# Moving two input loads and two dozen DRAM-to-DRAM copies in a decoder block: the embedding input ahead of the second merge gate, precomputed weight sums into the attention stages and late MLP1

## The chip, the cores and the metric

The kernel runs on one core of one Trainium2 chip. The metric is device time in microseconds (us) of one execution; lower is better.

## The reference, cut to what matters

One layer of a decoder trunk, batch 1, 512 tokens, width 1024, everything in float32:

```python
h = rmsnorm(x, ln1)
hq, hk, hv, hr, ha, hatt, hgate = split(h @ w_in)
# A: gated linear attention (4 heads, chunks of 64); B: dilated attention, 3 groups of 4 heads
o      = gla(...) * gla_gn * silu(hr);      y_gla = o @ w_o_gla
o_att  = softmax-weighted sum of 3 groups;  y_att = o_att @ w_o_attn
mix = (sigmoid(gA) * y_gla + sigmoid(gB) * y_att) @ w_out
x = x + mix
x = x + square(relu(rmsnorm(x, ln2) @ w_mlp1)) @ w_mlp2
x = x + sigmoid(rmsnorm(x, ln3) @ w_pg) * (p @ w_pp)
return rmsnorm(x, ln_f)
```

The last term but one, `p @ w_pp`, is the embedding product: `p` (512 x 256) does not depend on anything else, and its transpose is the input `pT`.

## The kernel before, in words

**Products.** Every weight is cut into operands of 128 x 1024 floats (512 KB). A product in full precision is made of three float32r matmuls: each operand and each activation is split into a high part (`hi`, rounded by ScalarE) and a low part (`lo` = value - hi, on VectorE), and hi*hi, hi*lo and lo*hi are added up in PSUM. Nearly all products are done by a seven-product scheme (Strassen-Winograd): `strassen` for the narrow ones and `wide` for the wide ones, where each of the seven stages has a sum of weight blocks (A11, S1, S2, A12, S3, S4, A22) and a sum of activation blocks (B11, T1, T2, B21, T3, B22, T4) as its operands. In `wide` each weight sum comes in two operands (`.0`, `.1`) of twelve matmuls each.

**Stages.** TensorE works through this order: q0, k0, q1, k1, q2, k2 (attention scores), v12, v0 (attention values), gq, gk, gv (linear attention), oa (attention output), r (the silu gate), gb and ga (the first and the second merge gate), og (`w_o_gla`, the linear-attention output projection), pp0 (first half of `p @ w_pp`), wo (`w_out`), pp1, m1q0 to m1q7 (MLP1), m2 (MLP2), pg. Attention, linear attention and other small work is woven in between matmuls.

**Order of the work.** The order in which instructions are issued is written out by hand: `tc.manual_schedule()` keeps each engine's instructions in program order. `run` emits matmuls in pieces, and after each piece `step` takes one closure from the list `later` (work on ScalarE and VectorE, first in, first out; `rest` is an empty one) and, at a pace, one turn of a generator from `side`. So an entry in `later` decides where a piece of work stands in the queues of ScalarE and VectorE.

**Weights.** `fetch` keeps two operands ahead of TensorE: for operand i it makes `lo`, for i+1 `hi`, and for i+3 it calls `prepare`, which issues the load on SyncE's queue (line 263). A weight sum that isn't a plain block is made by the transfers: a load, and then an accumulating transfer on GpSimd's queue that adds a second block (line 273, and in the product chains line 358). The accumulating transfer waits for the load and holds up what stands behind it in GpSimd's queue. In og the chain is S1, then S2 (S1 plus A11), then S4 (S2 plus A12), each by an accumulating transfer on the buffer whose low part has been made.

**Stored sums.** Twelve of MLP2's weight sums (S1 of four chunks, S3 of two, two operands each) are made ahead of time in DRAM: `store` copies a block from DRAM to DRAM on SyncE's queue (line 284) and `accumulate` adds the second block on GpSimd's queue (line 287). The generator `stores()` spreads them over 23 turns: two copies, then a copy and an accumulation in turn (each accumulation two sums behind its copy), then two accumulations. `prepare` takes a turn at every third operand of v12 and from gk on, which ends within gb.

**Embedding inputs.** After ga and ahead of og, two 128 x 512 tiles of `pT` are loaded on GpSimd's queue (line 1487), and two entries that split them are put into `later` (line 1489). pp0 reads the split tiles after og.

**Tiles.** All 128 x 512 work tiles come from one pool of 68 buffers (`NU`); `u32()` takes one.

Of the kernel before, what the change touches and what calls it, by code (L numbers as in the profile page):

```python
# [19 lines left out]
P = 128  # L20
# [112 lines left out]
def wide_order(name):  # L133
    return TIGHT if name in TIGHTS else WIDE


def operand_order():

    names = []
    for name, kind, *_ in UNITS:  # L140
        if name == f"m2c{SEVEN[0]}.A11.0":
            names += [f"m2c{c}.{a}.{i}" for a, c in MLP2 for i in range(2)]
        elif name.startswith("m2c"):
            continue
        elif kind not in QUADS:
            names.append(name)
        elif name.endswith("A11"):
            names += [f"{name[:-3]}{a}" for a, _, _ in STAGES]
        elif name.endswith("A11.0"):
            names += [f"{name[:-5]}{a}.{i}" for a, _, _ in wide_order(name[:-6]) for i in range(2)]  # L150
    return names
# [10 lines left out]
OPERANDS = operand_order()  # L162
OPERAND = {n: i for i, n in enumerate(OPERANDS)}
# [30 lines left out]

GOPS, LAG = 4, 3

PAD, SHIFT = 128, 32

NRAW = 8
# [9 lines left out]
def block_kernel(ctx, tc, xT, x, ws, pT, wts, wha, wa2, vec, lnf, rel, onehot, ident_d, mask_d, out):  # L209
    nc = tc.nc  # L210
    V, S, TE, SY, GP = nc.vector, nc.scalar, nc.tensor, nc.sync, nc.gpsimd
# [12 lines left out]
    def u32(name="u"):  # L224
        return ar.tile([P, T], F32, tag="u", name=name)
# [11 lines left out]
    side, later = [], []  # L237
# [28 lines left out]
    def prepare(i):  # L266

        name = OPERANDS[i]
        if i % 3 == 0 and (OPERAND["v12.A11.0"] <= i < OPERAND["v0.A11"] or i >= OPERAND["gk.A11"]):
            next(spare[0], None)  # L270
        for n, a, b in EARLY.get(i, ()):
            w = raw[n] = load(a)
            GP.dma_start(w, wts[UNIT[b]], accum_op=OP.add)  # L273
        if name in UNIT or name in stored:
            raw[name] = load(name)
# [28 lines left out]
    spare = [stores()]  # L304
# [82 lines left out]
    def cols(t, c):  # L387
        return t[0][:, c], t[1][:, c]
# [8 lines left out]
    def tmaj(name, n, lhs, evac, tts=range(4), piece=PIECE, last=None, make=mmt, at=None):  # L397

        last = tts[-1] if last is None else last

        for i in range(n):
            weight(f"{name}.{i}", 0)
        for tt in tts:
            ps = make()
            mms = three(ps, [(lhs(k, tt), cols(ready[f"{name}.{k // 2}"], slice((k % 2) * 512, (k % 2 + 1) * 512)))
                             for k in range(2 * n)])
            if at:
                run(mms, piece)
                fetch(OPERAND[f"{name}.{n - 1}"] + at[tt])
            elif tt != last:  # L410
                run(mms, piece)
            else:
                for i in range(n):
                    run(mms[6 * i:6 * i + 6], piece)
                    fetch(OPERAND[f"{name}.{n - 1}"] + i + 1 + (NW - 2 - n if n < 4 else 0))
            evac(tt, ps)
# [48 lines left out]
    def wide(name, xo, finish, base=None, piece=3, extra=None, first=False):  # L465


        bank, sums = {}, {}

        def begin(m, t, n, b):  # L470
            def go():
                if base:
                    return base(m, t, n, bank[b][n], sums)
                sums[m, t, n] = u32()
                S.activation(sums[m, t, n], bank[b][n], AF.Copy, scale=-1.0 if m else 1.0)
            return go

        def end(m, t, n, b):
            return lambda: finish(m, t, n, sums.get((m, t, n)), bank[b][n])

        for i, (op, xname, b) in enumerate(wide_order(name)):
            fresh = b not in bank
            if fresh:
                bank[b] = [smt() if b == "b" else mmt() for _ in range(2)]

            def products(n, pr):
                wh, wl = weight(f"{name}.{op}.{pr // 2}")
                xh, xl = xo(xname, pr)
                c, r = slice(n * P, (n + 1) * P), slice((pr % 2) * 512, (pr % 2 + 1) * 512)
                return [(bank[b][n], l[:, c], w[:, r], fresh and not pr and not k, pr == 3 and k == 2)  # L490
                        for k, (l, w) in enumerate(((xh, wh), (xl, wh), (xh, wl)))]

            begins = [begin(*BEGINS[op][0], n, BEGINS[op][1]) for n in range(2)] if op in BEGINS else []
            if name in TIGHTS and op in ("S2", "S3"):
                for n in range(2):
                    for pr in range(4):
                        run(products(n, pr), piece, shared=True)
                    later[0:0] = begins[n:n + 1]
            else:
                for pr in range(4):  # L500
                    run(products(0, pr) + products(1, pr), piece, shared=True)
                later[0:0] = begins
            if op in ENDS:
                (m, t), d = ENDS[op]
                ends = [end(m, t, n, d) for n in range(2)]
                if first:
                    later[0:0] = ends
                else:
                    later.extend(ends)
            if extra:  # L510
                extra(i)
# [21 lines left out]
    def split(x, col=None):  # L533

        return split_lo(x, split_hi(x, col), col)
# [62 lines left out]
    for k in range(KC):  # L598
        t = u32()
        SY.dma_start(t, xT[k * P:(k + 1) * P, :])  # L600
        xr.append(t)
        t = u32()
# [231 lines left out]
    def whole(m, s, ps):  # L834

        if s is None:
            s = u32()
            S.activation(s, ps, AF.Copy, scale=-1.0 if m else 1.0)
        else:
            add(m, s, s, ps)  # L840
        return s
# [495 lines left out]
    q2 = heads("q2", HD_SCALE, True)  # L1337
# [7 lines left out]
    v0 = values("v0")  # L1345
# [3 lines left out]
    gk = heads("gk", 1.0)  # L1349
    gv = {}  # L1350
# [11 lines left out]
    def evac_oa(j):  # L1362
        def put(tt, ps):
            y = u32()
            S.activation(y, ps, AF.Copy)
            S.dma_start(y_dram[4 * j + tt], y)
        return lambda tt, ps: later.append(lambda: put(tt, ps))

    for j in range(2):
        tmaj(f"oa{j}", 2, lambda k, tt: cols(oa[k], slice(tt * P, (tt + 1) * P)), evac_oa(j), at=((1, 1, 2, 2), (1, 2, 2, 3))[j])  # L1370
    rg, tb, ga = {}, {}, {}

    def silu(m, t, n, s, ps):
        s, g = whole(m, s, ps), u32()

        def act():
            S.activation(g, s, AF.Sigmoid)

            def mult():
                V.tensor_tensor(s, s, g, op=OP.mult)  # L1380
                rg[m, 2 * t + n] = s
            later.append(mult)
        later.append(act)

    def sigmoid(res):

        def finish(m, t, n, s, ps):
            if s is None:
                o = u32()
                S.activation(o, ps, AF.Sigmoid, scale=-1.0)  # L1390
                res[m, t, n] = o
            else:
                add(m, s, s, ps)

                def act():
                    S.activation(s, s, AF.Sigmoid)
                    res[m, t, n] = s
                later.append(act)

        return finish  # L1400
# [39 lines left out]
    def room(i):  # L1440
        if i >= 4:
            limit[0] += 1

    wide("ga", xs_op, sigmoid(ga), extra=room)
    limit[0] = 99
    pace[0], ways[0] = 2048, WAYS

    def rest():
        pass

    def og_op(name, pr):
        while (name, 1) not in gparts.op:
# [3 lines left out]
    def arrange(m, t, src, blk, parts, names, rests, col=None):  # L1456

        if (m, t) == (1, 1):
            return
        later.extend([rest] * rests[m, t] + turned(src, blk, m, t, col))  # L1460
        if t:
            later.extend(turned(src, blk, 1, 1, col))
        later.extend(parts.splits([(name, g) for name in names[m, t] for g in range(2)], LAG))
# [3 lines left out]
    mixed = {}  # L1467
# [13 lines left out]
            arrange(m, t, mixed, mblk, mparts, {(0, 0): ["B11"], (0, 1): ["T1", "T2"], (1, 0): ["B21", "T3", "B22", "T4"]},  # L1481
                    {(0, 0): 12, (0, 1): 7, (1, 0): 9})

    pt = []
    for k in range(2):
        t = u32()
        GP.dma_start(t, pT[k * P:(k + 1) * P, :])
        pt.append(t)
    later.extend(lambda k=k: pt.__setitem__(k, split(pt[k])) for k in range(2))
    wide("og", og_op, onto_mix, piece=2, first=True)  # L1490

    pp_dram = dr.tile([2 * 4, P, T], F32, name="pp_dram")
# [70 lines left out]
    def quad(q):  # L1563


        def finish(m, t, s, ps):
            add(m, s, s, ps)

            def positive():
                V.tensor_scalar(s, s, 0.0, None, op0=OP.max)  # L1570

            def act():
                S.activation(s, s, AF.Square)  # L1573
                hb[q, m, t] = s

            later.extend([positive, act])

        strassen(f"m1q{q}", x1_op, finish, extra=between(q))
# [42 lines left out]

    for q in range(8):
        quad(q)
    lnb, rt3 = [], []
    x3, ss3 = {}, const.tile([P, 8], F32, name="ss3")

# [168 lines left out]
    for c in parts:  # L1795
        ps, n = mmt(), c.stop - c.start
# [99 lines left out]
```

## Time and profile before

| | |
|---|---|
| median of three runs | 943.84 us (943.05 to 944.71) |
| the profiled execution | 944.67 us, its span from first to last instruction 942.9 us |
| TensorE's mean granted clock | 0.994 |
| matmul (PE) busy | 928.4 us, 98% of the span |
| VectorE busy | 745.9 us, 79% |
| ScalarE busy | 581.3 us, 62% |
| GpSimd busy | 142.3 us, 15% |
| data moved by DMA | 183.87 MB, mean 195 GB/s |

Engines are PE (TensorE's matmuls), PEld (its weight loads), DVE (VectorE), ACT (ScalarE), POOL (GpSimd) and SP (SyncE, which issues DMAs). A row of the timeline gives start, length, engine, line, operation, tiles written and read, shape and count; in brackets stands the idle time of the engine before it, and what ended that. A row of the windows gives, for one stretch, the busy time of PE, PEld, DVE, ACT and POOL with the instruction counts, then the granted clock, the share of the 16 DMA engines that was busy, and GB/s.

### The profile page before, as it was taken

To read this page: it belongs to the slowest core of one execution; us is meant where nothing else is said; L and a number is where in the kernel's file an instruction comes from. 1 tells how busy PE (TensorE), PEld (TensorE's weight loads), DVE (VectorE), ACT (ScalarE), POOL (GpSimd) and SP (SyncE) were. 2 spreads that over 40 slices of the span, in tenths; PEclk is the share of its full clock that TensorE was granted. 3 is DMA by queue.
4 is the path that set the end of the run, shared out by engine and by line. 5 is a ranking of instruction groups with operands and counts; after the bars stand their busy time and mean duration, and the time that the engine had idled before them with its cause. 6 is when DMAs were issued, how large, how long until landed. Compare 5 with 4: busy or idle time off the path is not lost.

```text
span 942.9 us, 14591 instructions
## 1 busy us (share of the span) xinstructions
PE 928.4 (98%) x5506; PEld 822.4 (87%) x5506; DVE 745.9 (79%) x1049; ACT 581.3 (62%) x939; POOL 142.3 (15%) x187
## 2 busy tenths in 40 slices
PE   9999999999999999999979999999999999999996
PEld 8789998899998888888868889999999888888886
DVE  7698879866789388977958989877768978899764
ACT  7357546545675578887655759755556665656543
POOL 0150020030201022133112120010000112120000
PEclk9999999999999999999989999999999999999999
DMA  9574685876867959599979696656654888897302
GB/s 346 151 235 113 195 223 119 276 251 190 181 154 224 278 132 302 114 226 260 256 201 236 195 257 192 188 143 165 174 150 121 198 191 197 189 287 286 112 0 90
DMA packets 59526, 183.87 MB, mean 195 GB/s; under 512 B 7875, under 2 KB 14607, under 8 KB 59264
## 3 DMA queue, kind: packets, MB, share of 16 engines
q0 software_dynamic: 23424, 65.24, 36.2%
q1 hardware_dynamic: 32352, 113.20, 33.6%
q10 hardware_dynamic: 3680, 4.51, 1.3%
q8 instruction: 43, 0.70, 0.3%
q14 instruction: 27, 0.22, 0.1%
HBM read 174.49 MB, written 22.85 MB: 209 GB/s over the span
## 4 chain that ended last, share of the span: by engine, by line
PE 90%; DMA 4%; ACT 2%; DVE 2%; issue 1%; POOL 0%; POOLq 0%; DVEq 0%; SPq 0%; ACTq 0%
PE mmt L377 68%; PE smt L377 13%; PE mmt L646 2%; DMA y_dram<-u 2%; PE smt L1080 1%; DMA u<-in_pT_dram 1%; DMA w<-in_wts_dram 1%; PE smt L1305 1%; PE smt L1020 1%; PE smt L943 1%; PE smt L913 0%; PE smt L1037 0%; PE smt L1036 0%; PE smt L912 0%; PE smt L1026 0%
## 5 line engine op out<-in xcount | busy, mean ns | idle before, releaser
L377 PE MATMUL mmt<-hi,ur 128*128 128x512 f32 (+1 forms) x1264 | 376.8, 381 | 0.0
L340 DVE TENSOR_TENSOR lo<-w,hi 128x1024 fp32r<-128x1024 f32 x266 | 322.5, 1219 | 57.6 <-PE mmt L377 31.9
L363 ACT ACTIVATE hi<-w 128x1024 fp32r<-128x1024 f32 x266 | 277.6, 1054 | 90.2 <-PE mmt L377 23.2
L377 PE MATMUL mmt<-ur,hi 128*128 128x256 f32 (+1 forms) x1552 | 294.7, 290 | 0.0
L377 PEld LDWEIGHTS mmt<-hi,ur 128*128 128x128 f32 x1264 | 230.5, 189 | 41.3
L377 PEld LDWEIGHTS mmt<-ur,hi 128*128 128x128 f32 x1552 | 244.3, 189 | 4.2
L377 PE MATMUL mmt<-lo,ur 128*128 128x512 f32 (+1 forms) x632 | 240.3, 380 | 4.9 <-DVE lo L340 4.9
L377 PE MATMUL mmt<-ur,lo 128*128 128x256 f32 (+1 forms) x776 | 225.8, 291 | 0.0
L377 PEld LDWEIGHTS mmt<-ur,lo 128*128 128x128 f32 x776 | 146.5, 189 | 1.9
L377 PEld LDWEIGHTS mmt<-lo,ur 128*128 128x128 f32 x632 | 119.3, 189 | 27.8 <-DVE lo L340 5.6
L523 ACT ACTIVATE ur<-u 128x512 fp32r<-128x512 f32 x137 | 80.9, 626 | 61.9 <-DVE u L665 12.5
L340 DVE TENSOR_TENSOR ur<-u,ur 128x512 fp32r<-128x512 f32 x136 | 89.0, 685 | 21.8 <-ACT ur L523 21.4
L377 PE MATMUL smt<-hi,ur 128*128 128x512 f32 x320 | 99.5, 392 | 0.0
L273 POOL DMA_DIRECT2D w<-in_wts_dram x46 | 46.0, 1073 | 220.8 <-DMA w<-in_wts_dram 92.7
L516 DVE TENSOR_TENSOR u<-u,mmt 128x512 f32<-128x512 f32 (+1 forms) x90 | 55.6, 646 | 23.6 <-PE mmt L377 23.4
L377 PEld LDWEIGHTS smt<-hi,ur 128*128 128x128 f32 x320 | 60.1, 189 | 12.2
L377 PE MATMUL smt<-lo,ur 128*128 128x512 f32 x160 | 62.6, 391 | 0.0
L450 ACT ACTIVATE u<-mmt 128x512 f32<-128x512 f32 x56 | 33.2, 594 | 47.1 <-PE mmt L377 46.9
L358 POOL DMA_DIRECT2D w<-in_wts_dram x28 | 25.0, 893 | 179.0 <-DVE lo L340 89.7
L319 POOL DMA_DIRECT2D w<-in_wts_dram x14 | 12.5, 894 | 212.3 <-DVE w L316 113.4
L1573 ACT ACTIVATE u<-u 128x512 f32<-128x512 f32 x32 | 20.1, 628 | 32.3 <-DVE u L1570 32.3
L377 PEld LDWEIGHTS smt<-lo,ur 128*128 128x128 f32 x160 | 30.2, 189 | 6.6 <-DVE lo L340 0.3
(239 smaller groups left out, 871.3 us busy)
## 6 DMA issues: line engine op xcount, KB each, us to landing
w<-in_wts_dram SPq DMA_DIRECT2D x176, 512.0 KB, 5.8
w<-in_wts_dram POOLq DMA_DIRECT2D x88, 512.0 KB, 7.6
m2c_S<-in_wts_dram SPq DMA_DIRECT2D x12, 512.0 KB, 8.4
m2c_S<-in_wts_dram POOLq DMA_DIRECT2D x12, 512.0 KB, 10.8
w<-m2c_S SPq DMA_DIRECT2D x12, 512.0 KB, 4.4
u<-in_xT_dram SPq DMA_DIRECT2D x8, 256.0 KB, 5.4
u<-in_ws_dram SPq DMA_DIRECT2D x8, 256.0 KB, 5.5
v_dram<-u ACTq DMA_DIRECT2D x8, 256.0 KB, 7.0
```

What stands on the lines that cost most here:

```text
L273: GP.dma_start(w, wts[UNIT[b]], accum_op=OP.add)
L319: GP.dma_start(w, wts[UNIT[f"{q}.A21"]], accum_op=OP.add)
L340: V.tensor_tensor(lo, x, hi.bitcast(F32), op=OP.subtract)
L358: GP.dma_start(w, wts[UNIT[f"{q}.{c}{what[2:]}"]], accum_op=OP.add)
L363: S.activation(hi[:, s], w[:, s], AF.Copy, scale=1.0 if c is None else c)
L377: TE.matmul(o, lhsT=l, rhs=r, start=a, stop=b, skip_group_check=shared)
L450: S.activation(sums[c], bank[b], AF.Copy, scale=-scale if c[0] else scale)
L516: V.tensor_tensor(out, s, ps, op=OP.subtract if m else OP.add)
L523: S.activation(hi, x, AF.Copy)
L646: TE.matmul(q0ps[i], lhsT=(hi, hi, lo)[j][:, c], rhs=(xh, xl, xh)[j], start=not k and not j, stop=k == KC - 1 and j == 2)
L943: TE.matmul(pss[b // 2][:, a * 256 + lo:a * 256 + 256], lhsT=q0[h][:, b * P:(b + 1) * P], rhs=k0[h][:, (b - 1) * P + lo:(b + 1) * P], star ...
L1573: S.activation(s, s, AF.Square)
```

## The change

- The two loads of `pT` are issued as ga, the second gate, begins, in place of og's beginning. Their splits are put into `later` when og's block (1, 1) has been finished, that is behind og's fifth stage, S3; they were ahead of og.
- The turns of `stores()` are taken at other operands. A table gives a modulus for some stages, and an operand takes a turn where its number leaves a remainder of 1. Stages that are not in the table have the modulus 275, one more than the number of operands, so that one more operand takes a turn: number 1 (`k0.1`). What is left when MLP1 has been issued is issued then.
- In the silu gate `r`, the tile for the sigmoid is taken when the sigmoid is issued, and not when the block is finished. `rest` is defined earlier, which moves no instruction.

```diff
+SPARE = {"q2": 2, "v12": 3, "gk": 2, "gv": 2, "m1q4": 3, "m1q5": 2, "m1q6": 2}
...
     def prepare(i):
 
         name = OPERANDS[i]
-        if i % 3 == 0 and (OPERAND["v12.A11.0"] <= i < OPERAND["v0.A11"] or i >= OPERAND["gk.A11"]):
+        if i % SPARE.get(name.partition(".")[0], len(OPERANDS) + 1) == 1:
             next(spare[0], None)
...
     def silu(m, t, n, s, ps):
-        s, g = whole(m, s, ps), u32()
+        s = whole(m, s, ps)
 
         def act():
+            g = u32()
             S.activation(g, s, AF.Sigmoid)
...
+    pt = []
+    for k in range(2):
+        t = u32()
+        GP.dma_start(t, pT[k * P:(k + 1) * P, :])
+        pt.append(t)
     wide("ga", xs_op, sigmoid(ga), extra=room)
...
     def arrange(m, t, src, blk, parts, names, rests, col=None):
 
         if (m, t) == (1, 1):
+            if src is mixed:
+                later.extend(lambda k=k: pt.__setitem__(k, split(pt[k])) for k in range(2))
             return
...
-    pt = []
-    for k in range(2):
-        t = u32()
-        GP.dma_start(t, pT[k * P:(k + 1) * P, :])
-        pt.append(t)
-    later.extend(lambda k=k: pt.__setitem__(k, split(pt[k])) for k in range(2))
     wide("og", og_op, onto_mix, piece=2, first=True)
...
     for q in range(8):
         quad(q)
+    for _ in spare[0]:
+        pass
```

More of the change, by code (lines that the diff above doesn't have):

```diff
@@ L1370, in block_kernel, with rest @@
         tmaj(f"oa{j}", 2, lambda k, tt: cols(oa[k], slice(tt * P, (tt + 1) * P)), evac_oa(j), at=((1, 1, 2, 2), (1, 2, 2, 3))[j])
+    def rest():
+        pass
     rg, tb, ga = {}, {}, {}
     def silu(m, t, n, s, ps):
-        s, g = whole(m, s, ps), u32()
+        s = whole(m, s, ps)
         def act():
+            g = u32()
             S.activation(g, s, AF.Sigmoid)
@@ L1446, in block_kernel @@
     pace[0], ways[0] = 2048, WAYS
-    def rest():
-        pass
     def og_op(name, pr):
@@ L1623, in block_kernel @@
         quad(q)
+    for _ in spare[0]:
+        pass
     lnb, rt3 = [], []
```

## The prediction

> **What bounds the kernel now.** I read the page's engine table and clock slices first, then TensorE's waits, then windows of 20 us.
>
> ```profile
> PE 928.4 (98%) x5506; PEld 822.4 (87%) x5506; DVE 745.9 (79%) x1049; ACT 581.3 (62%) x939; POOL 142.3 (15%) x187
> PEclk9999999999999999999989999999999999999999
> ...
> PE mmt L377 <- DVE lo L340: 4.9, 1, 4.9
> PE smt L615 <- POOL ones L610: 1.0, 1, 1.0
> PE smt L1130 <- DVE u L1110: 0.7, 1, 0.7
> PE smt L1080 <- DVE ur L1143: 0.5, 1, 0.5
> ...
> 460.00:480.00 20.00, 20.00 (x90) 16.57 (x89) 13.93 (x18) 12.16 (x18) 3.73 (x5) 1.00 0.97 282
> 480.00:500.00 20.00, 15.13 (x56) 11.98 (x55) 14.41 (x18) 11.69 (x16) 4.36 (x5) 0.83 0.76 168
> ```
>
> TensorE is the bound nearly everywhere. Between its start and its tail it waits three times: 4.9, 0.7 and 0.5 us. So a change can win only there, or lose by making a new wait. The long wait sits in 480 to 500, where TensorE got through 56 matmuls and not 90 of the same kind, at a mean clock of 0.83. Its cause, followed backwards in the timelines of PE, DVE, ACT and POOL, with the landing of the two loads and two rows of 1 us windows:
>
> ```profile
> 486.05 0.80 PE L377 MATMUL mmt<-lo,ur 128*128 128x512 f32 x1 [4.87 <-DVE lo L340]
> ...
> 484.77 1.22 DVE L340 TENSOR_TENSOR lo<-w,hi 128x1024 fp32r<-128x1024 f32 x1
> 481.75 1.90 DVE L340 TENSOR_TENSOR ur<-u,ur 128x512 fp32r<-128x512 f32 x3 [7.31 <-ACT ur L523]
> ...
> 481.09 1.67 ACT L523 ACTIVATE ur<-u 128x512 fp32r<-128x512 f32 x3 [6.67 <-DMA u<-in_pT_dram]
> ...
> 469.56 1.44 POOL L1487 DMA_DIRECT2D u<-in_pT_dram  x2
> DMA to landing us min/median/max: 11.4/11.4/11.5
> ...
> 485.00:486.00 1.00, 0.00 (x0) 0.00 (x0) 1.00 (x2) 1.00 (x2) 0.00 (x0) 0.50 0.00 0
> 491.00:492.00 1.00, 1.00 (x5) 0.82 (x4) 0.00 (x0) 0.00 (x0) 0.15 (x1) 0.81 0.96 332
> ```
>
> The `pT` loads are issued at 469.56 and land 11.4 us later, in a stretch where the DMA share is 0.97. ScalarE stands at the first split of `pT` for 6.67 us, VectorE behind it for 7.31, and og's next low part (S1.1, queued behind) ends at 485.99; TensorE had been out of work since 481.2. The clock fell to half and came back only at about 491.2.
>
> **Part 1: the loads moved ahead of ga.** The wait goes. Its price by counting: 34 matmuls fewer at 20/90 = 0.222 us, 7.6 us. By parts: 4.87 us idle, and 5.2 us (486.05 to 491.2) at half clock, which loses 2.6: 7.5. I take 7.5. [...]
>
> What is late next where the stall goes? Without it og.S1.1's low part follows VectorE's last work before the hole, which ends at 474.44 (first row below), so at about 476, some 5 us ahead of its matmul. Then comes og's own chain of accumulating transfers:
>
> ```profile
> 473.76 0.68 DVE L674 SCALAR_TENSOR_TENSOR u<-u 128x512 f32<-128x512 f32 x1
> ...
> 473.82 0.90 POOL L358 DMA_DIRECT2D w<-in_wts_dram  x1 [2.81 <-DVE lo L340]
> 486.53 0.87 POOL L358 DMA_DIRECT2D w<-in_wts_dram  x1 [11.81 <-DVE lo L340]
> DMA to landing us min/median/max: 5.4/6.9/10.1
> ...
> 498.21 0.39 PE L377 MATMUL mmt<-lo,ur 128*128 128x512 f32 x1
> ```
>
> The transfer that turns S1.1 into S2.1 went out at 486.53; it would now go at about 476. With the longest landing seen there, 10.1, it is in at 486, high and low part are made by 488.5, and TensorE, now 7.5 us earlier, first needs S2.1's low part at 498.2 - 7.5 = 490.7. Two us to spare: nothing by my count, up to 1 us of stall if a landing takes 13.
>
> The moved loads themselves (two issues, 1.44 us of POOL for both) stand in GpSimd's queue behind ga.S3's transfers and ahead of the transfer for ga.S4:
>
> ```profile
> 438.83 0.89 POOL L358 DMA_DIRECT2D w<-in_wts_dram  x1 [9.68 <-DVE lo L340]
> ...
> PEld mmt L377 <- DVE lo L340: 0.3, 1, 0.3
> ...
> q0 software_dynamic: 23424, 65.24, 36.2%
> q1 hardware_dynamic: 32352, 113.20, 33.6%
> ```
>
> GpSimd is idle for 9.68 us there, so its queue takes the issues for nothing. The bytes do not come quite free: queue 0 moved 65.24 MB in 36.2% of 942.9 us, 191 GB/s, so 512 KB cost 2.7 us of all DMA engines, among the loads of `y_dram` that the gate's merges wait for. In ga a low part is just in time (the wait of 0.3 us at about 453). A bound from above is thus 2.7 us of stall; from below, nothing or a small gain, since gb's five turns of stored sums (four accumulations of 512 KB each on queue 0, one copy) have left the stretch ahead of it. I take 0, as the two cancel. The two tiles are now held from ga to pp0, out of 68: that is the second unknown, in the rivals.
>
> **Part 2: the splits behind og's S3.** Two high parts on ScalarE, two low parts on VectorE. When block (1, 1) is finished, the entries in `later` are two finishes, two products, two sums and then the splits, so they come with the seventh and eighth of S4's twelve pieces, at about 511 to 514 of the old times; pp0 reads them at 519. ScalarE has holes there. VectorE has not:
>
> ```profile
> 505.92 1.29 DVE L340 TENSOR_TENSOR ur<-u,ur 128x512 fp32r<-128x512 f32 x2 [2.36 <-ACT ur L523]
> 520.00:540.00 20.00, 20.00 (x102) 16.88 (x101) 19.62 (x28) 16.47 (x28) 2.70 (x3) 1.00 0.60 189
> ...
> 526.57 1.29 DVE L1480 TENSOR_TENSOR u<-u 128x512 f32<-128x512 f32 x2
> 528.59 1.03 PE L1305 MATMUL smt<-ident,u 128*128 128x128 f32 x8
> ...
> 542.06 1.22 DVE L340 TENSOR_TENSOR lo<-w,hi 128x1024 fp32r<-128x1024 f32 x1
> 543.98 0.39 PE L377 MATMUL smt<-lo,ur 128*128 128x512 f32 x1
> ```
>
> After its pause at 505.9 VectorE runs nearly without a hole beyond 542. Two more low parts cost it 1.90/3 x 2 = 1.3 us, and what follows is that much later. Two readers have less room: the transposes at 528.59 (the sums end at 527.86: 0.7) and wo.A12's low part (ends 543.28, read at 543.98: 0.7). Stall: 1.3 - 0.7 = 0.6 us; it is one shift, and the first stall makes room for the second. Bounds: 0 if the pause at 505.9 grows less than TensorE's lead; 2 if each low part also waits for its high part.
>
> **Part 3: the stored sums.** Both plans have 23 turns. Before: v12 5, gk 3, gv 4, oa 2, r 4, gb 5. After: k0 1 (number 1 leaves remainder 1 by 275), q2 4, v12 4, gk 4, gv 7, m1q4 2, m1q5 1; nothing is left for the last loop. Copies and accumulations run beside TensorE, so only crowding can cost:
>
> ```profile
> 88.00:110.00 22.00, 22.00 (x178) 21.69 (x177) 20.48 (x31) 13.72 (x31) 0.86 (x1) 1.00 0.38 99
> 246.00:305.00 59.00, 59.00 (x359) 52.74 (x359) 50.05 (x71) 37.90 (x55) 5.67 (x7) 1.00 0.74 192
> 305.00:330.00 25.00, 25.00 (x126) 20.95 (x125) 10.32 (x16) 13.95 (x24) 3.39 (x4) 1.00 1.00 283
> 645.00:690.00 45.00, 45.00 (x377) 45.00 (x376) 31.01 (x36) 24.68 (x33) 3.51 (x4) 1.00 0.59 156
> ...
> 314.24 9.64 DMA y_dram<-u
> 324.59 5.66 DMA y_dram<-u
> ...
> 21.40 1.08 POOL L273 DMA_DIRECT2D w<-in_wts_dram  x1 [19.82 <-DMA w<-in_wts_dram]
> 28.84 1.04 POOL L548 TENSOR_TENSOR rtok<-rv,mh 128x4 f32<-128x4 f32 x1 [6.37 <-DVE rv L547]
> ```
>
> q2 (share 0.38) and m1q4 to m1q5 (0.59) have room for four and three transfers of at most 2.7 us: 0. gv gets three more: 8 us on 59, from 0.74 to 0.88: 0 taken, 2.7 (one transfer late) as the bound. At the start two copies go out between k0.0 and k0.1; at twice a load's time (queue 1: 357 GB/s, so 1.5 us, read and written) they delay k1's first accumulation by 6 us, from 21.4 to 27.4, and GpSimd is next wanted at 28.84: 0, bound 1. What leaves oa and r is a gain: at 305 to 330 the share is 1.00, and the chain of waits runs through the stores of `y_dram` (9.64 and 5.66 us), which hold ScalarE, then VectorE, up to the wait of 0.7 us at L1130. I take 0.7 for it; 0 is the other end.
>
> The later tile in `silu` moves no instruction; it may change which buffer is taken, price unknown, taken as 0.
>
> **The sum**, against the profiled execution: 944.67 - 7.5 + 0.6 - 0.7 = 937.1. That execution stood 0.8 above the median of 943.84, so 936.2 for the median.
>
> **The rivals.** (a) *A short new wait* (in gv, ga, or VectorE in wo): 2 to 4 us come back without the clock's loss, for the clock slices show no dip at the wait of 0.7 us. ga's 0.3 us wait speaks for it, the leads elsewhere against: 938 to 941. (b) *The change doesn't pay*: og's chain is late instead and the wait is as long as the old one. For it: the DMA share of 0.97; against: 2 us of room in the count above. 942.5 to 945. (c) *Slower*: the `pT` load waits in GpSimd's queue for a tile. The longest waits there reach tens of us:
>
> ```profile
> POOL w L273 <- DMA w<-in_wts_dram: 92.7, 8, 22.6
> ```
>
> Up to 9.7 us fit in the hole before 438.83; beyond that ga.S4's transfer is late, with some 3 us of lead, and each further us is a us of stall, with 2.6 of clock on top. It decides from a wait of about 18 us; at 22.6 the stall is 9.9 + 2.6 = 12.5 against 7.6 won: 949. Against it: `pT` waited for no tile at 469.56, and at ga's beginning r and the silu gate have given tiles back. (d) *More than I count*: 0.5 us at L1080 goes too, and VectorE's shift is absorbed: 934.5 to 935.2.
>
> **How the numbers follow.** My forecast (935.3 to 938) 0.60, (a) 0.18, (b) 0.08, (c) 0.07, (d) 0.07. The range leaves out (b), (c) and a little below: 934.8 to 941. 0.2% is 1.9 us, about what a measurement of this kernel can tell from no change: faster 0.84 (forecast, a, d), same 0.08 (b), slower 0.08.
>
> **What would show it.** Right: no wait of ScalarE on `in_pT_dram`, no clock digit under 9 at 480, `y_dram` stores in half the time, TensorE's waits at about 1 us after the start. Wrong: a wait of ScalarE or GpSimd on a tile in ga; a low part in og, wo or gv with TensorE waiting for it; GpSimd's queue standing still ahead of 439.

## The result, and the profile after

The changed kernel takes 936.50 us (median of 6 runs, 935.95 to 936.91), the kernel before 943.58 us beside it (6 runs, 943.05 to 944.71): a ratio of 0.9924, 95% interval 0.9911 to 0.9936. The forecast was 936.2. The profiled execution took 936.23 us with a span of 934.5 us.

From the page of the changed kernel, its waits of TensorE (us in total, times, longest), and its windows:

```profile
PE 925.0 (99%) x5506; PEld 820.1 (88%) x5506; DVE 746.7 (80%) x1049; ACT 582.2 (62%) x939; POOL 142.9 (15%) x187
PEclk9999999999999999999999999999999999999998
...
PE smt L617 <- POOL ones L612: 1.0, 1, 1.0
PE smt L1082 <- DVE ur L1145: 0.6, 1, 0.6
PE smt L379 <- DVE lo L342: 0.3, 1, 0.3
PE smt L1022 <- DVE u L1002: 0.2, 1, 0.2
...
305.00:330.00 25.00, 25.00 (x126) 20.93 (x125) 13.65 (x24) 14.39 (x26) 1.73 (x2) 1.00 0.75 225
460.00:480.00 20.00, 20.00 (x90) 16.57 (x89) 18.88 (x24) 15.31 (x23) 3.44 (x4) 1.00 0.96 278
480.00:500.00 20.00, 20.00 (x93) 16.62 (x93) 13.39 (x16) 12.80 (x17) 3.51 (x4) 1.00 1.03 253
```

The waits of 4.9 us and 0.7 us are gone; 0.6, 0.3 and 0.2 us are left behind the start. From 480 to 500 TensorE gets through 93 matmuls, where it got through 56, at a clock of 1.00 where it was 0.83, although the DMA engines are busier there (1.03, where it was 0.76). At 305 to 330 the share fell from 1.00 to 0.75.

The lines of the changed kernel stand 2 to 6 higher (L377 is L379, L340 is L342, L1487 is L1453, L1412 is L1418). Its timelines of POOL, DVE and PE at the places that the prediction names, with the landing of the two `pT` loads:

```profile
24.50 1.08 POOL L275 DMA_DIRECT2D w<-in_wts_dram  x1 [22.92 <-DMA w<-in_wts_dram]
...
424.75 1.45 POOL L1453 DMA_DIRECT2D u<-in_pT_dram  x2
425.86 2.48 POOL L1418 DMA_DIRECT2D u<-y_dram  x4
437.41 0.89 POOL L360 DMA_DIRECT2D w<-in_wts_dram  x1 [9.06 <-DVE lo L342]
...
DMA to landing us min/median/max: 7.4/7.4/7.5
...
449.37 0.69 DVE L1423 TENSOR_TENSOR u<-u 128x512 f32<-128x512 f32 x1 [1.91 <-DMA u<-y_dram]
452.46 0.50 PE L379 MATMUL smt<-lo,ur 128*128 128x512 f32 x1 [0.27 <-DVE lo L342]
...
477.01 0.86 POOL L360 DMA_DIRECT2D w<-in_wts_dram  x1 [3.62 <-ACT hi L365]
484.73 1.23 DVE L342 TENSOR_TENSOR lo<-w,hi 128x1024 fp32r<-128x1024 f32 x1 [1.78 <-ACT hi L365]
489.58 0.39 PE L379 MATMUL mmt<-lo,ur 128*128 128x512 f32 x1
...
504.38 1.29 DVE L342 TENSOR_TENSOR ur<-u,ur 128x512 fp32r<-128x512 f32 x2
534.10 5.76 DVE L342 TENSOR_TENSOR lo<-w,hi 128x1024 fp32r<-128x1024 f32 x5
535.38 0.50 PE L379 MATMUL smt<-lo,ur 128*128 128x512 f32 x1
```

`pT` now lands in 7.4 us, and nothing waits for it: its low parts are made 70 us later (504.38). In the row of 449.37 VectorE waits 1.91 us for a `y_dram` load, and TensorE loses 0.27 us to it. That load went out at 442.86, when `pT` had landed 10 us before, and with the sums alone moved VectorE waits 1.36 us at the same merge (449.00), so this wait isn't shown to come from `pT`; before it was 0.46 us.

Where the time went is read by pairing the 5506 matmuls of both traces in order. A matmul of the changed kernel starts earlier than the same one before by: 0.8 us from 7 us on; 0.6 from gk; 1.4 from r; 1.0 in ga; 8.6 in og once the clock would have come back; 8.4 from wo to the end. So og gave 7.6, r 0.8, the start 0.8, and gk, ga and wo took back 0.2, 0.4 and 0.2. (These are the gains of one execution over another; which of them the change made is a question for the experiments.)

### The profile page after: what moved, and what is told of

Same layout as the page of the kernel before. It is cut to its first block, busy times and chain, and to the rows that moved or that the text cites. A ratio compares the mean times of both kernels' runs of the same rounds, so it can differ in the third digit from the quotient of the medians.

```text
span 934.5 us, 14591 instructions
## 1 busy us (share of the span) xinstructions
PE 925.0 (99%) x5506; PEld 820.1 (88%) x5506; DVE 746.7 (80%) x1049; ACT 582.2 (62%) x939; POOL 142.9 (15%) x187
## 4 chain that ended last, share of the span: by engine, by line
PE 94%; ACT 2%; DVE 2%; issue 1%; DMA 1%; POOL 0%; POOLq 0%; DVEq 0%; SPq 0%; ACTq 0%
PE mmt L379 71%; PE smt L379 13%; PE mmt L648 2%; PE smt L1082 1%; PE smt L1307 1%; PE smt L1022 1%; DMA u<-y_dram 1%; PE smt L945 1%; PE smt L915 0%; PE smt L1039 0%; PE smt L1028 0%; PE smt L914 0%; PE smt L1038 0%; PE smt L1238 0%; ACT hi L365 0%
## 5 line engine op out<-in xcount | busy, mean ns | idle before, releaser
L379 PE MATMUL mmt<-hi,ur 128*128 128x512 f32 (+1 forms) x1264 | 375.6, 380 | 0.0
L342 DVE TENSOR_TENSOR lo<-w,hi 128x1024 fp32r<-128x1024 f32 x266 | 322.9, 1220 | 60.2 <-PE mmt L379 31.9
L379 PE MATMUL mmt<-ur,hi 128*128 128x256 f32 (+1 forms) x1552 | 294.6, 290 | 0.0
L379 PEld LDWEIGHTS mmt<-hi,ur 128*128 128x128 f32 x1264 | 229.6, 188 | 41.0
L379 PEld LDWEIGHTS mmt<-ur,hi 128*128 128x128 f32 x1552 | 244.1, 189 | 4.2
L379 PE MATMUL mmt<-lo,ur 128*128 128x512 f32 (+1 forms) x632 | 239.2, 378 | 0.0
L379 PE MATMUL mmt<-ur,lo 128*128 128x256 f32 (+1 forms) x776 | 225.9, 291 | 0.0
L379 PEld LDWEIGHTS mmt<-ur,lo 128*128 128x128 f32 x776 | 146.5, 189 | 2.0
L379 PEld LDWEIGHTS mmt<-lo,ur 128*128 128x128 f32 x632 | 118.8, 188 | 22.5 <-DVE lo L342 0.3
L379 PE MATMUL smt<-hi,ur 128*128 128x512 f32 x320 | 99.1, 390 | 0.0
L342 DVE TENSOR_TENSOR ur<-u,ur 128x512 fp32r<-128x512 f32 x136 | 89.2, 686 | 12.4 <-ACT ur L525 12.0
L275 POOL DMA_DIRECT2D w<-in_wts_dram x46 | 48.1, 1099 | 216.7 <-DMA w<-in_wts_dram 97.1
L379 PEld LDWEIGHTS smt<-hi,ur 128*128 128x128 f32 x320 | 59.8, 188 | 12.0
L379 PE MATMUL smt<-lo,ur 128*128 128x512 f32 x160 | 62.7, 392 | 0.3 <-DVE lo L342 0.3
L360 POOL DMA_DIRECT2D w<-in_wts_dram x28 | 24.6, 880 | 171.9 <-DVE lo L342 78.5
L321 POOL DMA_DIRECT2D w<-in_wts_dram x14 | 12.9, 918 | 202.5 <-issue 100.2
L379 PEld LDWEIGHTS smt<-lo,ur 128*128 128x128 f32 x160 | 30.0, 188 | 7.1 <-DVE lo L342 0.9
```

Source lines behind the costliest of these rows:

```text
L321: GP.dma_start(w, wts[UNIT[f"{q}.A21"]], accum_op=OP.add)
L342: V.tensor_tensor(lo, x, hi.bitcast(F32), op=OP.subtract)
L360: GP.dma_start(w, wts[UNIT[f"{q}.{c}{what[2:]}"]], accum_op=OP.add)
L379: TE.matmul(o, lhsT=l, rhs=r, start=a, stop=b, skip_group_check=shared)
```

## The experiments

### Each part alone

`e1_pt_only`: before, with the loads of `pT` ahead of ga and the splits behind S3; the sums and the silu tile as before.

```diff
+    pt = []
+    for k in range(2): ...   # load pT
     wide("ga", xs_op, sigmoid(ga), extra=room)
...
         if (m, t) == (1, 1):
+            if src is mixed:
+                later.extend(... split(pt[k]) ...)
             return
```

> The embedding input's loads ahead of ga and its splits behind og's S3; the stored sums and the silu tile as before. Theory (the wait for the load is nearly the whole gain): og's wait of 4.87 us and the half clock behind it go, 7.6 us; 0.2 us come back in wo, up to 0.4 in ga: 936.2 to 936.7, and the wait of 0.7 us at the key transposes in r stays. Rival (the sums that left r and gb made the room): og still waits, a gain of 4 us or less, 939 or more.

`e2_sums_only`: before, with the table of turns (`SPARE`) and nothing else.

> Only the stored sums are moved. Theory: the wait for the embedding input stays as it was (ScalarE about 6.7 us, TensorE 4.9 us, half clock), and 0.9 us are won where y_dram is stored ahead of r: 942.5 to 943. Rival (crowding by the sums is why that load takes 11.4 us): ScalarE's wait falls under 4 us and the time to 940 or less.

The kernel before took 943.68 us beside these two. The sums alone: 942.47 (941.63 to 944.67), ratio 0.9991 (0.9981 to 1.0000), about as expected; og's wait stays (TensorE 4.4 us, ScalarE 6.2 us for `pT`). The loads and splits alone: 942.11 (938.96 to 943.94), ratio 0.9976 (0.9964 to 0.9988), its runs spread over 5 us; expected was nearly the whole gain. My theory fell here: 1.6 and 1.2 us alone, 7.1 together. The waits, the window and the timelines of PE, DVE and POOL of the first kernel (`pT` alone moved) say where it went:

```profile
PE smt L377 <- DVE lo L340: 3.7, 2, 2.7
DVE u L1417 <- DMA u<-y_dram: 7.2, 3, 4.6
...
424.91 0.86 POOL L273 DMA_DIRECT2D w<-in_wts_dram  x1 [9.61 <-DVE u L1228]
428.79 0.87 POOL L273 DMA_DIRECT2D w<-in_wts_dram  x1 [3.02 <-DVE u L1228]
429.32 1.45 POOL L1447 DMA_DIRECT2D u<-in_pT_dram  x2
430.43 2.47 POOL L1412 DMA_DIRECT2D u<-y_dram  x4
...
441.15 0.69 DVE L1417 TENSOR_TENSOR u<-u 128x512 f32<-128x512 f32 x1 [4.62 <-DMA u<-y_dram]
457.60 0.75 PE L377 MATMUL smt<-lo,ur 128*128 128x512 f32 x1 [2.74 <-DVE lo L340]
...
480.00:500.00 20.00, 20.00 (x90) 16.58 (x89) 14.93 (x18) 11.33 (x15) 4.37 (x5) 1.00 1.02 235
```

og's wait is gone (90 matmuls from 480 to 500). But ga has a wait of its own: the `y_dram` loads go out at 430.43, behind `pT` and behind two accumulating transfers at 424.91 and 428.79 which had themselves stood for 9.61 and 3.02 us, VectorE waits 7.2 us for them in its merges, and TensorE 3.7 us for the low parts behind these. They went out 3.8 us later than before (426.64 there), of which `pT`'s two issues are 1.1 us.

### Half of the embedding part

`e3_loads_only`: the loads ahead of ga, the splits at og's beginning as before. `e4_splits_only`: the loads at og's beginning as before, the splits behind S3. Sums as before in both.

> The loads ahead of ga, the splits still at og's beginning, sums and silu tile as before. Theory: the wait goes, and without the two low parts in VectorE's full stretch wo's A12.0 keeps its lead of about 0.7 us: 936 to 936.5, og's S1.1 with a lead of 2 us or more. Rival (the place of the splits does it): TensorE still waits at og's S1.1, 938 or more.

> The splits behind og's S3, the loads still at og's beginning, sums and silu tile as before. Theory (only ScalarE's standing still mattered, not the bytes): the loads land at about 481, the splits come at about 504, no wait: 936 to 936.7. Rival (the 512 KB amid og's transfers cost by themselves): og's S2.1 or S4 is late by 1 to 3 us: 937.5 to 940.

Loads only: 939.89 us (938.97 to 941.81), ratio 0.9960 (0.9948 to 0.9972); no loss in og or wo, one wait of 2.2 us in ga. Splits only: 939.63 (939.07 to 941.83), ratio 0.9961 (0.9947 to 0.9974); no wait of 4.9 us, but og and wo lost some 2.4 us in small pieces. Neither reached the 936 to 937 us of its theory; splits only lies in its rival's 937.5 to 940. Waits of ScalarE and of TensorE in og and wo, of the second:

```profile
ACT hi L363 <- DMA w<-in_wts_dram: 9.5, 5, 3.3
PE smt L1305 <- DVE u L1482: 0.8, 3, 0.3
```

Either half alone takes the long wait away. The first leaves ga's new wait. In the second ScalarE waits for weights, at the longest 3.3 us, and TensorE for sums behind them; with six empty entries (below) the longest is 2.4 us and nothing is lost.

### What ga's new wait comes from

The second theory was that the five turns of stored sums left in gb crowd the loads and hold GpSimd's queue, so that `pT` ahead of the `y_dram` loads makes these late. `e5_gb_turns_out` is the first kernel (`pT` moved) with only those five turns moved, to m1q4 and m1q5. `e6_gb_turns_kept` is the changed kernel with only its last five turns put back into gb. `e8_loads_behind_y` is the first kernel with `pT` issued two stages later, behind the first four `y_dram` loads:

```diff
 # e5, e6: turns by number of the operand
+        if i in TURNS:
 # e8: in room()
+        if i == 1:
+            for k in range(2): ...   # load pT
```

> The embedding part as in the first experiment; of the stored sums only gb's five turns are moved, into m1q4 and m1q5; the silu tile as before. Theory 2 (gb's stored sums hold up GpSimd's queue, so that with the embedding loads ahead of them the loads of y_dram go out 4 us late, and VectorE waits in ga): ga's wait falls under 1 us, 937 to 938, that is the changed kernel less the 0.9 us won ahead of r. Rival (the other 18 turns or the silu tile make the difference): 940 to 942 as with the embedding part alone.

> The changed kernel, but its last five turns of stored sums stand in gb, at the operands where they stood before. Theory 2: VectorE waits 2 us or more for y_dram in ga again and TensorE 2 to 4 us: 939.5 to 942. Rival: 936.5, as the changed kernel.

> The embedding part alone, with the two loads issued after ga's second stage and so behind the first four loads of y_dram in GpSimd's queue; stored sums and silu tile as before. Theory 2 (order in the queue): the first loads of y_dram go out at about 427 as before, VectorE waits under 1.5 us, 937 to 938.5. Rival (the bytes themselves, in whatever order): waits for y_dram or og's transfers of 2 us or more, 939 to 942.

The kernel before took 943.99 us. Turns out of gb: 937.31 (936.74 to 939.47), ratio 0.9931 (0.9916 to 0.9946), no wait over 0.5 us behind the start. Turns kept in gb: 940.37 (939.46 to 940.83), ratio 0.9958 (0.9945 to 0.9971), with ga's wait back. `pT` behind `y_dram`: 939.10 (936.94 to 942.05), ratio 0.9945 (0.9926 to 0.9964), above the theory's 938.5 and in the rival's range; ga's wait is gone, but og and wo lose some 3 us in the places of the splits-only kernel, with a wait of ScalarE for a weight of 4.9 us. That `pT`'s bytes were paid for there isn't shown (see the silu tile). Waits of TensorE and VectorE and a row of POOL, first of the kernel with the turns kept, then VectorE's wait of the one with them out:

```profile
PE smt L381 <- DVE lo L344: 3.1, 2, 2.4
DVE u L1425 <- DMA u<-y_dram: 6.3, 3, 3.9
430.90 0.54 POOL L1420 DMA_DIRECT2D u<-y_dram  x1 [2.22 <-PE smt L1240]
```

```profile
DVE u L1419 <- DMA u<-y_dram: 1.8, 2, 1.5
```

In the first, one `y_dram` load also waits 2.22 us for a tile (TensorE's read of it): the two tiles that `pT` now holds may be missed there; no run frees them alone. Over all fourteen profiles ga divides by whether gb has its turns and whether `pT` is issued ahead of `y_dram`:

| | `pT` ahead of `y_dram` | `pT` later |
|---|---|---|
| turns in gb | TensorE's wait in ga 2.2, 3.1, 3.7 us; VectorE's for `y_dram` 5.7 to 7.2 | 0, 0, 0.4, 1.4 us; 1.8 to 4.5 |
| no turns in gb | 0, 0, 0, 0.3, 0.4 us; 1.4 to 2.4 | 0, 0 us; 1.5, 1.7 |

(The kernel with `pT` behind the first four `y_dram` loads is counted as later.) So in these profiles, one of each kernel, either alone costs TensorE at most 1.4 us in ga, and the two together 2 to 4 us, and more with the clock. (The 1.4 us are of the kernel with six empty entries, whose program up to og is that of before, with no wait there: so much differs from one execution to another.) The times agree: with `pT` ahead of ga, 937.31 us without the turns in gb, 942.11 with them; in the changed kernel's plan 936.50 and 940.37, their intervals apart. That the two together make the wait is thus shown. How it is made isn't, and it isn't the order in GpSimd's queue alone, as the second theory had it. With the turns kept in gb the first `y_dram` load went out 0.9 us later than in the changed kernel (426.76, 425.86), but took 12.0 us to land where it took 9.1. In the first kernel it went out 3.8 us later than before and took 10.7 where it took 9.8; there the accumulating transfers stood late (424.91, against 421.99 before) ahead of any load of `pT`.

### The silu tile

`e7_silu_as_before`: the changed kernel with both tiles taken at once again (`s, g = whole(m, s, ps), u32()`).

> The changed kernel with the silu tile taken as before. Theory 2: the tile does nothing, 936 to 937. Rival (one more tile held in r delays something): 938 or more, with a new wait in r or gb.

936.51 us (935.88 to 937.14), ratio 0.9919 (0.9906 to 0.9931): the tile does nothing that can be measured. Its profile shows how much one execution differs from another: it loses nothing in ga, but 1.4 us in og and wo, with a wait of ScalarE for a weight of 4.3 us. So these late weights come with `pT` loaded ahead of ga, too.

### What the changed kernel still owes to each move

`e9_loads_at_og` puts the loads back to og's beginning, `e10_splits_first` the splits, each in the changed kernel.

> The changed kernel with the two loads of pT back at og's beginning; the splits stay behind og's S3 and the stored sums stay moved. It asks whether the loads still have to move once nothing that TensorE needs stands behind their splits. Theory: moving the splits alone left losses of 2 to 3 us spread over og and wo, because 512 KB of pT among og's weight transfers make high parts late; the sums have nothing to do with that stretch, so 939.63 less what moving the sums alone brought (1.2) less ga's share of a fraction: 938.0 to 938.8, with small waits of TensorE in og and wo. Rival: those losses came from the same crowd that the sums have left, so the place of the loads no longer matters: 936.2 to 937.0.

> The changed kernel with the splits of pT back at og's beginning, loads ahead of ga and sums moved. Theory: the two subtractions no longer push VectorE in wo, which cost TensorE 0.2 us there in the changed kernel (a low part with 0.06 us to spare, 0.3 us of waiting weight loads); og has 3.6 us of lead at its tightest low part: 936.2 to 936.5, no wait of ScalarE on pT. Rival by the prediction's own term: 0.6 us comes back, 935.9. If the splits at og's beginning get in the way of og's high parts: 937 or more.

The kernel before took 944.33 us (942.08 to 946.75). With the loads at og: 937.92 (936.48 to 939.88), ratio 0.9934 (0.9918 to 0.9949). It lies just below the theory's 938.0, but runs differ by 3.4 us and its interval holds the changed kernel's ratio: as a median 1.4 us are lost, and that isn't told from none. With the splits at og's beginning: 935.86 (935.64 to 936.38), ratio 0.9911 (0.9897 to 0.9925). It is the fastest kernel seen, 0.6 us below the changed one by the medians, which the intervals don't separate; the theory had said 936.2 to 936.5, the prediction's own term 935.9. Its rows of DVE show that the splits hold up nothing there now: VectorE stands 0.52 us ahead of them, and og.S1.1's low part follows at 477.35 and is done at 478.57, 1.8 us before TensorE reads it (480.41):

```profile
474.33 1.90 DVE L342 TENSOR_TENSOR ur<-u,ur 128x512 fp32r<-128x512 f32 x3 [0.52 <-ACT ur L525]
477.35 1.22 DVE L342 TENSOR_TENSOR lo<-w,hi 128x1024 fp32r<-128x1024 f32 x1
```

`e11_six_subtractions` doubles the suspected cost of the late splits, and more: each low part of `pT` is subtracted three times.

```diff
+                def splits(k):
+                    pt[k] = split(x := pt[k])
+                    for _ in range(2):
+                        split_into(pt[k][1], x, pt[k][0], None)
-                later.extend(lambda k=k: pt.__setitem__(k, split(pt[k])) for k in range(2))
+                later.extend(lambda k=k: splits(k) for k in range(2))
```

> The changed kernel with each of the two subtractions that make pT's low parts done three times (same result): four more subtractions of 0.6 us on VectorE at about 504 us, 2.4 us more work. Theory: VectorE has no idle time from there to 538 us and wo.A12.0's low part 0.06 us to spare, so nearly all of it becomes stall of TensorE in wo: 1.8 to 2.4 us more, 938.3 to 938.9. Rival (the 1.2 us of the two splits were absorbed because the queue is elastic, so the place of VectorE's work near there hardly matters): at most 0.5 us more, 936.5 to 937.0.

939.79 us (939.27 to 943.36), ratio 0.9958 (0.9942 to 0.9973): 3.3 us slower than the changed kernel for 2.4 us of work, above the theory's 1.8 to 2.4 and far from the rival's 0.5. The timelines of DVE and PE:

```profile
504.90 4.20 DVE L342 TENSOR_TENSOR ur<-u,ur 128x512 fp32r<-128x512 f32 x6
512.55 1.29 DVE L1494 TENSOR_TENSOR u<-u 128x512 f32<-128x512 f32 x2
513.30 0.33 PE L1307 MATMUL smt<-ident,u 128*128 128x128 f32 x1 [1.27 <-DVE u L1494]
```

TensorE waits first at 513.30, for the transposes of a sum that follows the splits on VectorE; my theory had named only wo's low part at 535. So the place has little room: two subtractions fit, six don't.

`e12_six_rests` is the kernel before with one line added, six empty entries ahead of the two splits.

```diff
+    later.extend([rest] * 6)
     later.extend(lambda k=k: pt.__setitem__(k, split(pt[k])) for k in range(2))
     wide("og", og_op, onto_mix, piece=2, first=True)
```

> The kernel before with nothing moved but six empty entries put into the list ahead of pT's two splits, so that og.S1.1's low part stands ahead of them on VectorE and no longer behind. ScalarE still waits for pT for some 4 to 6 us. Theory: the 4.9 us wait goes, since what TensorE needs next is not behind the splits; what is left is og.A12.0's high part behind them on ScalarE (done about 482.5, low part 484, needed at 483.9), so at most 1 us of wait at a whole clock, and the bytes of pT in og's transfers cost 1 to 2 us as they did when the splits alone were moved: 938.0 to 939.6. Rival (a ScalarE that stands still for 5 us stops TensorE whichever low part is first): the wait moves one operand on and keeps most of its size, 941 to 943.

939.10 us (936.83 to 940.90), ratio 0.9944 (0.9927 to 0.9960), within what the theory said. The profiled execution took 937.79. Its rows of ACT and DVE, a window, and TensorE's one wait in ga and og:

```profile
479.51 0.63 ACT L523 ACTIVATE ur<-u 128x512 fp32r<-128x512 f32 x1 [1.33 <-DMA u<-in_pT_dram]
480.97 0.63 ACT L523 ACTIVATE ur<-u 128x512 fp32r<-128x512 f32 x1 [0.82 <-DMA u<-in_pT_dram]
...
477.08 1.22 DVE L340 TENSOR_TENSOR lo<-w,hi 128x1024 fp32r<-128x1024 f32 x1
...
480.00:500.00 20.00, 20.00 (x94) 16.62 (x93) 15.02 (x18) 13.67 (x21) 3.49 (x4) 1.00 1.02 242
...
PE smt L377 <- DVE lo L340: 1.4, 1, 1.4
```

og.S1.1's low part now stands ahead of the splits and starts at 477.08, not 484.77; ScalarE still waits for `pT`, 2.2 us, and TensorE doesn't notice (94 matmuls from 480 to 500). The 1.4 us are in ga. So the long wait was one of order in two queues: six empty entries, with no load and no sum moved, bring some 5 of the 7 us by the medians. It also shows that `pT`'s bytes among og's weights need not cost anything in og: in this execution they didn't, in the splits-only kernel they did. The kernel with the silu tile as before lost time there with `pT` loaded ahead of ga. What made the weights late stays open.

## Why the prediction was right, and where it wasn't

- **Part 1, the wait in og.** Forecast 7.5, found 7.6. og's chain of transfers did as counted: the transfer for S2.1 went out at 477.01 (forecast 476), its low part ended at 485.96, and TensorE read it at 489.58: 3.6 us to spare, not 2, because it landed sooner than the 10.1 us that I had allowed (the longest landing there was 8.0). The half clock ended at 491.38 by the window's mean, so it lasted 5.3 us after the work resumed, not 5.2; that changes nothing in the 7.5.
- **"I take 0, as the two cancel".** ga lost 0.4 us in this execution and nothing in that of the kernel with the silu tile as before, so the 0 was right as a sum. But the step holds only as a whole: the cover was gb's five turns leaving, and with them in place the same loads came with 2.2 to 3.7 us of wait in three kernels. I had named this cover and its price, a bound of 2.7, but as bytes; with the half clock on top the first kernel lost 5.5 us there (3.7 of wait and half of the 3.5 us from 457.60 to 461.10), twice that. Parts 1 and 3 don't add up: the sum has 7.5 and 0.7, each alone gives 1.6 and 1.2.
- **Part 2, VectorE in wo.** Forecast 0.6, found 0.2. VectorE was pushed by 1.2 us, about as counted (1.3), but holes ahead of wo took about half, and the low part of wo.A12.0 (the first of the five from 534.10, done at 535.32) came 0.06 us ahead of its matmul. A mis-sized term: the shift was taken whole, less the one slack of 0.7.
- **Part 3, the sums.** oa and r gave 0.8 (taken 0.7), by the way that was forecast: the first four stores of `y_dram` took a median of 5.0 us to land where they took 8.6, and the wait of 0.7 us is gone. With the sums alone moved r gives the same (0.9). The copies at the start moved k1's first accumulation from 21.40 to 24.50, not to 27.4, and cost nothing. In gk and gv 0.2 us of wait is new (L1022), taken as 0.
- **The sum against the profiled execution.** -7.6 - 0.8 + 0.4 + 0.2 + 0.2 makes -7.6 where I had -7.6: errors of a few tenths cancel. The profiled execution fell by 8.4, and the 0.8 more is luck at the start, which I had set aside as its distance from the median without knowing where it lay. By 7.5 us TensorE had begun eight matmuls of this line in the execution of before and eleven in the changed one (first and second row):

```profile
4.93 2.89 PE L646 MATMUL mmt<-ur 128*128 128x512 f32 x8 [0.15 <-DVE ur L631]
4.91 2.76 PE L648 MATMUL mmt<-ur 128*128 128x512 f32 x11 [0.21 <-DVE ur L633]
```

Before, they start some 0.43 us apart until 6.7 us, the distance seen in the half clock behind 486.05 (though the granted clock reads 1.00 from 5 to 6 us), and 0.23 us apart from then on. It isn't the change: in the kernels that start just as the one before it had begun 7 to 11 by then. By the medians, which this touches less, the gain is 7.1 us.

- **The rivals.** (a), a short new wait in ga, is what comes when gb keeps its turns, at the 938 to 941 it gave or above (940.37, 942.11). But its reason for no loss of clock was wrong: waits of 2.4 and 2.7 us halved the clock (below). (c)'s wait for a tile exists, 2.2 us of it, on a `y_dram` load and not on `pT`.

## What to carry to other kernels

When an engine stands at a late input, look first at what is queued behind that wait, not at the input: letting the next needed operand pass took one line here and most of the gain. When a load is moved earlier in an in-order queue, count the time of what it is put ahead of, and what else crowds that stretch; two moves that bring 7 us together brought 3 one by one here, so they are judged together. After a fix, look at every lead that is left before more work is put there: the tightest was 0.06 us here, but the next piece of work stalled TensorE first at an earlier reader that had had 1 us.

## What the runs showed of the hardware that I had not expected

The half clock went on for 3.0 to 5.3 us after TensorE had work again. Windows at its two ends, in this order: before (its end at 491 stands in the prediction), the `pT`-only kernel, and the one with the turns kept in gb:

```profile
484.00:485.00 1.00, 0.00 (x0) 0.00 (x0) 1.00 (x3) 0.71 (x2) 0.00 (x0) 0.78 0.00 0
```

```profile
457.00:458.00 1.00, 0.40 (x1) 0.40 (x2) 1.00 (x2) 1.00 (x3) 0.00 (x0) 0.84 0.97 320
461.00:462.00 1.00, 1.00 (x5) 0.78 (x5) 1.00 (x2) 0.00 (x0) 0.00 (x0) 0.95 0.60 57
```

```profile
455.00:456.00 1.00, 0.70 (x2) 0.61 (x3) 1.00 (x3) 1.00 (x2) 0.00 (x0) 0.56 0.80 295
458.00:459.00 1.00, 1.00 (x5) 0.79 (x4) 1.00 (x2) 0.58 (x1) 0.35 (x1) 0.73 0.13 49
```

A mean clock of 0.78 between 1.0 and 0.5 puts the change at 484.56; so the half clock lasted from 484.56 to 491.38 before (6.82 us), 457.68 to 461.10 (3.42) and 455.12 to 458.54 (3.42). With the sums alone it lasted from 483.80 to 487.21 (3.41), by means of 0.90 from 483 to 484 and 0.89 from 487 to 488. Work had come back at 486.05, 457.60, 455.30 and 484.19, and the full clock 5.3, 3.5, 3.2 and 3.0 us later. Why the half clock lasted twice as long before as in the other three isn't shown.

The waits that halved the clock were 4.9 us (before), 4.4 (the sums alone), 2.7 and 2.4 us (the two other kernels). One of 2.2 us in the loads-only kernel left it whole (1.00 in every us from 453 to 459), and so did one of 1.4 us with six empty entries (1.00 from 440 to 460). What decides it between 2.2 and 2.4 us, the length of the wait or something else, isn't shown.

So the price of a wait jumped here: one of 2.4 us lost some 1.6 us more to the half speed (3.24 us of work, from 455.30 to 458.54), one of 2.2 us nothing.
